# An RWKV kernel on one core: output matrices built on VectorE, head loads on SyncE, and a re-placed end of the state chain

## The chip, the core and the metric

The kernel runs on one core of a Trainium2 chip. A core has a matrix engine (TensorE, PE in the profile; its weight loads are shown as PEld), VectorE (DVE), ScalarE (ACT), GpSimd (POOL) and SyncE (SP). Each engine works through its own queue in order, and the engines wait for each other by semaphores. SP, ACT and POOL can issue DMAs. The metric is the device time of one execution in microseconds; lower is better.

## What is computed

A recurrence over time runs for each of 16 sequences of 2048 steps and each of 256 channels. `k` and `v` are 16 x 2048 x 256 floats (33.5 MB each), and so is the output.

```python
for t in range(seq_len):
    ww = u + kk                       # kk = k[b,t], vv = v[b,t]
    qq = np.maximum(pp, ww)
    e1 = np.exp(pp - qq); e2 = np.exp(ww - qq)
    output[b, t] = (e1 * aa + e2 * vv) / (e1 * bb + e2 + 1e-08)
    ww = pp - w + kk
    qq = np.maximum(ww, kk)
    e1 = np.exp(ww - qq); e2 = np.exp(kk - qq)
    aa = e1 * aa + e2 * vv
    bb = e1 * bb + e2
    pp = qq
```

The output is a decayed sum of values (the numerator) over a decayed sum of weights (the denominator); `aa`, `bb` and `pp` carry the state.

## The kernel before

**Tiling.** 2048 = 32 + 16 x 126. The first 32 steps of all sequences are "the head"; the rest are 16 steps of time, c = 0 to 15, of 126 rows each (two halves of 63). A tile has the time on its partitions. The work is cut into 66 pairs: a pair is one step of time of 4 sequences (two matrix tiles of 512 columns). Pairs 0 and 1 belong to step 0, pairs 2 and 3 are the head (pair 3 is half as large), pairs 4 and 5 finish step 0, and then there are four pairs for each step: pairs 58 to 61 are step 14, pairs 62 to 65 are step 15.

**One pair.** Its K and V are loaded (`load`, 512 KB each; four buffers of each). DVE casts K (`round_k`, writing `km`, L285). PE multiplies it by two constant matrices (`logs`, L301, writing `X`), ACT takes exponentials (`exps`, L317, writing `ez`), V is cast to bf16 (`cast_v`; on ACT for pairs 2 to 7, L326, otherwise on DVE, L328), DVE multiplies `ez` by V (`times_v`, L336), and PE adds up columns (`sums`, L366, writing `tot`). Ten rounds later (six for the head) comes the output of the pair: PE makes denominators (`den`, L512) and numerators (`num`, L534) with the constant matrices `Lf`, `Id`, `LfN`, `IdN` (`Lh`, `LhN` for the head); ACT takes the logarithm of the denominators (`log_den`, L521) and the exponential of its negative (`invert`, L526); DVE multiplies (`mult`, L542); and a DMA stores the tile (`store`, L562). From pair 8 on `X` has one buffer of four PSUM banks, so `logs` of the next pair waits for `exps` of this one.

**The state chain.** When the four pairs of a step are summed, a chain of small instructions turns sums into the carries of that step: ACT copies `tot` (`copy_sums`, `ts`), PE transposes it (`turn_sums`, L382), DVE copies that (`split_sums`, `tsum`, L389), ACT takes logarithms (`state_logs`, `lf`, L401), DVE adds and clamps them (`state_offset`, L406; `state_near`, `near`, L410), ACT makes weights from these (`state_weights`, `w` and `g`, L420 and L421), DVE updates the state (`state_sums`, `state_add`, `state_decay`), ACT makes two more small functions (`inject_logs` `y`, L455; `inject_weights` `phi`, L461), DVE forms the carries (`carry_weights`, `carries` `ab`, L466 and L473), PE transposes them (`turn_carries`, L479, with the matrix `It`), DVE copies them (`row`, L484), and SP sends them by four small DMAs of 8 KB into two spare rows of `ez` (`inject`, L488). Denominators and numerators of the step's pairs read these rows.

**The order.** The order on each engine is the order in which the program is written: the helper `K` pins each instruction behind the one before it on its engine. The main loop has rounds n = 0 to 77; in round n it does `exps`, `times_v` and `sums` of pair n, the cast and `logs` of pair n + 1, `den` and `log_den` of pair q = n - 10, `invert` of n - 11, and `num`, `mult` and `store` of n - 12. Between these stand named slots (`a0` to `a4`, `d0` to `d5`, `p0` to `p4`), where `small_work` puts pieces of the state chain and of the set-up; a table `PLANS` says for each kind of step, counted in rounds from its last pair, which piece goes into which slot. Slot `a3` is ahead of `exps(n)`, `d5` and `a1` stand at the end of a round, `d2` behind the first `mult`. From round 66 on there are no new pairs, and `widen` gives the freed PSUM banks to denominators (two buffers) and numerators (three).

**Set-up.** POOL makes the base matrices `M1` and `I1`. From these POOL also builds the output matrices, in three batches, at the ends of rounds 3, 4 and 5 (L253 to L256, L260 to L263, L267 to L273), between the loads that it issues. Loads of pairs 0 and 1 are on SP, those of pairs 4 and later on POOL, four pairs ahead. The head's loads are small pieces of 32 rows, K on SP and V on POOL (L129). All stores are on POOL, but for the second half of the last pair's, on SP.

Of the kernel before, what the change touches and what calls it, by code (L numbers as in the profile page):

```python
# [7 lines left out]
F32 = mybir.dt.float32  # L8
F32R = mybir.dt.float32r
BF16 = mybir.dt.bfloat16  # L10
ALU = mybir.AluOpType
# [11 lines left out]
def kernel(  # L23
# [11 lines left out]
    def K(ins):  # L35

        block, e, new = nc.cur_bb.bb, ins.ins.engine, []
        for i in reversed(block.instructions):
            if i.engine == e:
                new.append(i)  # L40
                if i.name == pinned.get(e):
                    break
        for a, b in zip(new[1:], new):
            tc.add_manual_dep(b, a.name, mybir.DependencyInfo(
                mybir.DependencyClass.NoSync, mybir.DependencyReason.DATA), reason="order")
        pinned[e] = new[0].name
# [12 lines left out]
    NH = NG * GB  # L59
# [5 lines left out]
    RS = 2.0 ** -43  # L65
# [30 lines left out]
    NP = len(pairs)  # L96
# [17 lines left out]
    def load(n):  # L114
        kr = kpool.tile([128, 4, Dm], F32, tag="kr", name="kr")
        vr = vpool.tile([128, 4, Dm], F32, tag="vr", name="vr")
        kr_of[n], vr_of[n] = kr, vr
        c, p = pairs[n]
        if is_head(n):
            if p == 1:  # L120
                K(POOL.memset(kr[64:96, 0:2, :], 0.0))
                K(POOL.memset(vr[64:96, 0:2, :], 0.0))

            for t, x, eng, groups in ((kr, k, SP, range(NG)), (vr, v, POOL, reversed(range(NG)))):
                for g in groups:
# [26 lines left out]
    def matrix(name, dt, width=128):  # L152
        return consts.tile([128, width], dt, tag=name, name=name)
# [7 lines left out]
    def fill(ap, value):  # L161
        K(DVE.memset(ap.bitcast(F32) if ap.dtype == F32R else ap, value))
# [3 lines left out]
    cc = matrix("cc", F32, 8)  # L166
# [18 lines left out]
    def head_blocks(f):  # L185
        fill(f[0:GB, GB:NH], 0.0)
        fill(f[GB:2 * GB, 2 * GB:NH], 0.0)
# [62 lines left out]

    def matrices_for_outputs():

        K(POOL.tensor_copy(It, I1))  # L253
        K(POOL.tensor_copy(Id, I1))
        K(POOL.tensor_copy(Id[:, TC:128], I1[:, TC - 1:TC].broadcast_to([128, 128 - TC])))
        K(POOL.tensor_scalar(IdN, Id, RS, None, ALU.mult))  # L256

    def matrices_for_outputs_of_head():
        for t, s in ((Lh, 1.0), (LhN, RS)):
            K(POOL.tensor_scalar(t, M1, -s, None, ALU.mult))  # L260
            K(POOL.memset(t[0:GB, GB:NH], 0.0))
            K(POOL.memset(t[GB:2 * GB, 2 * GB:NH], 0.0))
            K(POOL.memset(t[:, NH:128], 0.0))  # L263

    def more_matrices_for_outputs():
        Lx = matrix("Lx", F32)
        K(POOL.tensor_scalar(Lx, M1, -1.0, None, ALU.mult))  # L267
        K(POOL.memset(Lx[0:HS, HS:TC], 0.0))
        K(POOL.tensor_scalar(Lx[:, 0:HS], Lx[:, 0:HS], cc[:, 2:3], None, ALU.add))
        K(POOL.tensor_scalar(Lx[:, HS:TC], Lx[:, HS:TC], cc[:, 3:4], None, ALU.add))  # L270
        K(POOL.tensor_copy(Lx[:, TC:128], Lx[:, TC - 1:TC].broadcast_to([128, 128 - TC])))
# [235 lines left out]
    def den(n):  # L507
        rl, ri = (NH, NH) if is_head(n) else (128, TC)
        d = bank("den", [128, 2, D])
        for m, r, q in (((Lh if is_head(n) else Lf), rl, 0), (Id, ri, 2)):  # L510
            for i in range(tiles_of(n)):
                K(PE.matmul(d[:, i, :], m[0:r, :], ez_of(n)[0:r, q, i, :], start=q == 0, stop=q == 2,  # L512
                            skip_group_check=True))
        DEN[n] = d
# [29 lines left out]
    def store(n):  # L544
        o = RD.pop(n).rearrange("p i (n d) -> p (i n) d", n=2)
        if n % 2 == 1:
            EZ.pop(n // 2)
        if is_head(n):
            for g in range(NG):
                b = 6 * g + 4 * pairs[n][1]  # L550
                e = min(b + 2 * tiles_of(n), B)
                if b < e:
                    K(POOL.dma_start(out=out[b:e, 0:T0, :].rearrange("n t d -> t n d"),
                                     in_=o[g * GB:(g + 1) * GB, 0:e - b, :]))
        else:
# [18 lines left out]
    def small_work(n, where):  # L574
        for f, args in later.pop((n, where), []):
            f(*args)
# [13 lines left out]
                   (3, "d4", state_decay, 0), (4, "a0", inject_logs), (4, "a2", inject_weights),  # L590
                   (4, "d4", carry_weights), (4, "d5", carries), (4, "p4", turn_carries), (5, "d0", inject),
                   (5, "d2", state_add, 1), (5, "d4", state_decay, 1)),
        "last": ((1, "a0", copy_sums), (1, "p1", turn_sums), (1, "p1", split_sums), (1, "a2", state_logs),
                 (1, "d5", state_offset, 0), (1, "d5", state_offset, 1), (1, "d5", state_near),
                 (1, "a1", state_weights), (2, "d0", state_sums), (2, "d0", state_add, 0),
                 (2, "d0", state_decay, 0), (2, "a2", inject_logs), (2, "a2", inject_weights),
                 (2, "d2", carry_weights), (2, "d2", carries), (2, "p2", turn_carries), (2, "d5", inject)),
    }
    for c in range(-1, NST):
        for slot, where, f, *args in PLANS["head" if c < 0 else "first" if c == 0 else  # L600
                                           "last" if c + 1 == NST else "steady"]:
# [12 lines left out]
    for n in range(NP + LAG + 2):  # L614

        q, qi, qp = out_at.get(n), out_at.get(n - 1), out_at.get(n - 2)
        live, more, out_q, out_qi, out_qp = n < NP, n + 1 < NP, q is not None, qi is not None, qp is not None
        if n == NP:
            widen()
        if n + AHEAD < NP:  # L620
            load(n + AHEAD)
        small_work(n, "a3")
        if live:
            exps(n)
        small_work(n, "d0")
# [75 lines left out]
```

## Time and profile before

| | |
|---|---|
| times of five runs | 323.63, 324.89, 325.53, 327.46, 330.95 us |
| median | 325.53 us |
| the profiled execution's own time | 323.63 us |
| its span, first to last instruction | 321.9 us |
| mean granted TensorE clock | 0.978 |
| moved by DMA | 102.96 MB, 320 GB/s over the span |

The profile is of the fastest of the five runs; 1.7 us of its time lie outside the span. In the rows of the profile a label such as L512 is a line of the kernel, `out<-in` are tile names, and a bracket at the end gives how long the engine had been idle before and what ended that. PEclk is the granted TensorE clock in tenths.

### The profile page before, as it was taken

What the parts mean: (1) busy time and instruction counts of PE and PEld (TensorE: products, weight loads), DVE (VectorE), ACT (ScalarE), POOL (GpSimd) and SP (SyncE); (2) the same over time, 40 slices, a digit from 0 to 9 for tenths busy, and PEclk for the clock granted to TensorE, in tenths of its full rate; (3) what the DMA queues carried; (4) which work ended last, traced back from release to release, by engine and by line L of the source; (5) the groups of instructions that cost most, each with busy time, mean ns of one, the idle gap of its engine ahead of it and who ended that gap; (6) DMA issues with size and microseconds to landing.
All of it is one profiled execution on the core that took longest, in us unless ns stands there. A gap on an engine that the chain in (4) does not pass through costs nothing. (4 is left out here: it accounts for less than half of the span.)

```text
span 321.9 us, 3974 instructions
## 1 busy us (share of the span) xinstructions
PE 281.1 (87%) x1132; PEld 126.4 (39%) x1132; DVE 277.6 (86%) x546; ACT 278.3 (86%) x318; POOL 179.2 (56%) x249
## 2 busy tenths in 40 slices
PE   1699779799999999999999999999999999997980
PEld 1334334254444444344444344444434444432430
DVE  4847877989999999999999999999999999977670
ACT  6589689599898999989898989899998989986990
POOL 8778917564466655556664646665555664112331
PEclk9999799999999999999999999999999999997995
DMA  6999798999999999999999999999999999944775
GB/s 205 245 349 350 227 340 243 328 337 320 344 348 356 377 359 363 352 365 365 372 357 347 375 360 368 363 374 357 347 370 369 368 318 279 312 166 155 246 250 171
DMA packets 33743, 102.96 MB, mean 320 GB/s; under 512 B 6638, under 2 KB 9482, under 8 KB 33722
## 3 DMA queue, kind: packets, MB, share of 16 engines
q0 software_dynamic: 27616, 99.27, 90.1%
q1 hardware_dynamic: 6074, 3.42, 4.2%
q8 instruction: 9, 0.15, 0.2%
q14 instruction: 12, 0.10, 0.1%
q10 hardware_dynamic: 32, 0.02, 0.0%
HBM read 68.12 MB, written 34.05 MB: 317 GB/s over the span
## 5 line engine op out<-in xcount | busy, mean ns | idle before, releaser
L562 POOL DMA_DIRECT2D out_dram<-rd x64 | 53.8, 841 | 121.3 <-issue 48.3
L317 ACT ACTIVATE ez<-X 128x2048 bf16<-128x2048 f32 x58 | 108.6, 1873 | 8.7 <-PE num L534 6.7
L542 DVE TENSOR_TENSOR rd<-num,rd 128x512 f32<-128x512 f32 (+2 forms) x131 | 88.9, 685 | 15.8 <-ACT rd L526 6.7
L336 DVE TENSOR_TENSOR ez<-ez,vb 126x2048 bf16<-126x2048 bf16 (+1 forms) x66 | 79.7, 1207 | 6.4 <-ACT ez L315 5.8
L521 ACT ACTIVATE rd<-den 128x1024 f32<-128x1024 f32 (+3 forms) x67 | 67.0, 1000 | 16.5 <-PE den L512 16.1
L526 ACT ACTIVATE rd<-rd 128x1024 f32<-128x1024 f32 (+3 forms) x67 | 69.3, 1034 | 0.3
L301 PE MATMUL X<-km,NLE 128*128 128x512 f32 x128 | 52.2, 490 | 10.2 <-DVE km L285 6.5
L135 POOL DMA_DIRECT2D kr<-in_k_dram x62 | 56.5, 912 | 2.5 <-DVE km L285 1.4
L534 PE MATMUL num<-ez,LfN 128*128 128x512 bf16 x128 | 49.6, 388 | 4.4 <-DVE rd L542 0.8
L534 PE MATMUL num<-ez,IdN 126*128 126x512 bf16 (+1 forms) x131 | 50.3, 384 | 0.0
L135 POOL DMA_DIRECT2D vr<-in_v_dram x62 | 48.6, 785 | 2.5 <-ACT vb L326 1.6
L328 DVE CAST vb<-vr 126x1024 bf16<-126x1024 f32 x60 | 46.6, 776 | 0.8 <-DMA vr<-in_v_dram 0.7
L366 PE MATMUL tot<-ez,OHV 126*48 126x512 bf16 x128 | 39.3, 389 | 7.7 <-DVE ez L336 6.3
L285 DVE CAST km<-kr 126x1024 fp32r<-126x1024 f32 x64 | 43.9, 687 | 1.9 <-DMA kr<-in_k_dram 1.9
L301 PE MATMUL X<-km,NLZ 128*128 128x512 f32 x128 | 41.4, 406 | 0.4 <-ACT ez L315 0.2
L512 PE MATMUL den<-ez,Lf 128*128 128x512 bf16 x128 | 38.5, 382 | 2.4 <-DMA ez<-row 1.6
L366 PE MATMUL tot<-ez,OHE 128*48 128x512 bf16 x128 | 40.5, 399 | 0.0
L512 PE MATMUL den<-ez,Id 126*128 126x512 bf16 (+1 forms) x131 | 39.4, 381 | 0.0
L301 PEld LDWEIGHTS X<-km,NLE 128*128 128x128 f32 x128 | 23.8, 192 | 22.3 <-DVE km L285 6.5
L301 PEld LDWEIGHTS X<-km,NLZ 128*128 128x128 f32 x128 | 24.6, 194 | 7.4 <-ACT ez L315 1.7
L366 PEld LDWEIGHTS <-OHV 126*48 126x48 bf16 x128 | 13.5, 105 | 30.2 <-issue 21.5
L534 PEld LDWEIGHTS <-LfN 128*128 128x128 bf16 x128 | 12.4, 97 | 28.9 <-issue 26.0
(111 smaller groups left out, 215.1 us busy)
## 6 DMA issues: line engine op xcount, KB each, us to landing
out_dram<-rd POOLq DMA_DIRECT2D x60, 512.0 KB, 7.1
kr<-in_k_dram POOLq DMA_DIRECT2D x58, 512.0 KB, 8.1
vr<-in_v_dram POOLq DMA_DIRECT2D x58, 512.0 KB, 8.6
kr<-in_k_dram POOLq DMA_DIRECT2D x4, 504.0 KB, 10.3
vr<-in_v_dram POOLq DMA_DIRECT2D x4, 504.0 KB, 11.0
out_dram<-rd POOLq DMA_DIRECT2D x3, 504.0 KB, 4.3
kr<-in_k_dram SPq DMA_DIRECT2D x2, 512.0 KB, 5.0
vr<-in_v_dram SPq DMA_DIRECT2D x2, 512.0 KB, 7.8
```

The lines of the kernel that those rows point to most:

```text
L135: K((SP if n < 2 else POOL).dma_start(out=t[0:r, :, :], in_=x[4 * p:4 * p + 4, t0:t0 + r, :].rearrange("n t d -> t n d")))
L301: K(PE.matmul(X[q][:, i, :], m[0:kr, :], km[0:kr, i, :], start=True, stop=True))
L317: K(SC.activation(ez_of(n)[:, 0:4:2], X[2][:, :, 0:i, :], ACT.Exp))
L328: K(DVE.tensor_copy(vb[0:r, 0:i, :], vr_of.pop(n)[0:r, 0:i, :]))
L336: K(DVE.tensor_mul(ez[0:r, 1:4:2], ez[0:r, 0:4:2], vb[0:r, 0:i, :].unsqueeze(1).broadcast_to([r, 2, i, D])))
L366: K(PE.matmul(TOT[c], m[0:r, :], ez_of(n)[0:r, q, i, :], start=n == first_of[c] and i == 0 and q == 0, stop=n == last_of[c] and i == tiles ...
L512: K(PE.matmul(d[:, i, :], m[0:r, :], ez_of(n)[0:r, q, i, :], start=q == 0, stop=q == 2, skip_group_check=True))
L521: K(SC.activation(RD[n][0:r, a:b, :], DEN[n][0:r, a:b, :], ACT.Ln, scale=RS))
L526: K(SC.activation(RD[n][0:r, a:b, :], RD[n][0:r, a:b, :], ACT.Exp, scale=-1.0))
L534: K(PE.matmul(d, m[0:r, :], ez_of(n)[0:r, q, i, :], start=q == 1, stop=q == 3, skip_group_check=True))
L542: K(DVE.tensor_mul(RD[n][0:r, i, :], NUM.pop((n, i))[0:r, :], RD[n][0:r, i, :]))
L562: K(eng.dma_start(out=out[4 * p + a:4 * p + b, t0:t0 + r, :].rearrange("n t d -> t n d"), in_=o[0:r, a:b, :]))
```

## The change

Four things change.

1. The output matrices are built on DVE instead of POOL, at the same places of the loop (ends of rounds 3, 4 and 5), with 15 instructions instead of 19; the float32 stage `Lx` is gone.
2. The head's loads all go to SP, K and then V of pair 2, K and then V of pair 3.
3. In the state chain, step 14 has a plan of its own ("before"), mostly one round earlier than "steady" had it: the copy of sums at the end of round 62, `lf` ahead of `exps(63)`, the carries sent in round 65. In the plan of step 15 ("last") offsets and `near` come behind the first product of round 66 instead of the second, and the carries' weights, the carries and their transposition at the end of round 67, behind both products and the denominators.
4. In round 66 the second numerator comes behind `turn_sums`; in round 67 the denominators of pair 58 come directly behind those of pair 57. The store of pair 64 goes to SP.

```diff
-            for t, x, eng, groups in ((kr, k, SP, range(NG)), (vr, v, POOL, reversed(range(NG)))):
-                for g in groups:
+            for t, x in ((kr, k), (vr, v)):
+                for g in range(NG):
...
-                        K(eng.dma_start(out=t[g * GB:(g + 1) * GB, 0:e - b, :],
+                        K(SP.dma_start(out=t[g * GB:(g + 1) * GB, 0:e - b, :],
...
     def matrices_for_outputs():
-        K(POOL.tensor_copy(It, I1))
-        K(POOL.tensor_copy(Id, I1))
-        K(POOL.tensor_copy(Id[:, TC:128], I1[:, TC - 1:TC].broadcast_to([128, 128 - TC])))
-        K(POOL.tensor_scalar(IdN, Id, RS, None, ALU.mult))
+        K(DVE.tensor_copy(It, I1))
+        K(DVE.tensor_copy(Id[:, 0:TC], I1[:, 0:TC]))
+        K(DVE.tensor_copy(Id[:, TC:128], I1[:, TC - 1:TC].broadcast_to([128, 128 - TC])))
+        K(DVE.tensor_single_scalar(IdN, Id, RS, op=ALU.mult))
     def matrices_for_outputs_of_head():
-        for t, s in ((Lh, 1.0), (LhN, RS)):
-            K(POOL.tensor_scalar(t, M1, -s, None, ALU.mult))
-            K(POOL.memset(t[0:GB, GB:NH], 0.0))
-            K(POOL.memset(t[GB:2 * GB, 2 * GB:NH], 0.0))
-            K(POOL.memset(t[:, NH:128], 0.0))
+        K(DVE.tensor_single_scalar(Lh, M1, -1.0, op=ALU.mult))
+        head_blocks(Lh)
+        fill(Lh[:, NH:128], 0.0)
+        K(DVE.tensor_single_scalar(LhN, Lh, RS, op=ALU.mult))
     def more_matrices_for_outputs():
-        Lx = matrix("Lx", F32)
-        K(POOL.tensor_scalar(Lx, M1, -1.0, None, ALU.mult))
...
-        K(POOL.tensor_copy(Lf, Lx))
-        K(POOL.tensor_scalar(LfN, Lx, RS, None, ALU.mult))
+        K(DVE.tensor_single_scalar(Lf, M1, -1.0, op=ALU.mult))
+        fill(Lf[0:HS, HS:TC], 0.0)
+        K(DVE.tensor_scalar(Lf[:, 0:HS], Lf[:, 0:HS], cc[:, 2:3], None, ALU.add))
+        K(DVE.tensor_scalar(Lf[:, HS:TC], Lf[:, HS:TC], cc[:, 3:4], None, ALU.add))
+        K(DVE.tensor_copy(Lf[:, TC:128], Lf[:, TC - 1:TC].broadcast_to([128, 128 - TC])))
+        K(DVE.tensor_single_scalar(LfN, Lf, RS, op=ALU.mult))
...
-            for a, b, eng in ((0, 2, POOL), (2, 4, SP)) if n == NP - 1 else ((0, 4, POOL),):
+            for a, b, eng in ((0, 2, POOL), (2, 4, SP)) if n == NP - 1 else ((0, 4, SP if n == NP - 2 else POOL),):
...
+        "before": ((1, "a0", copy_sums), (1, "p2", turn_sums), (1, "d5", split_sums), (2, "a3", state_logs),
+                   (2, "d1", state_offset, 0), (2, "d2", state_offset, 1), (2, "d3", state_near),
+                   (2, "a1", state_weights), (3, "d0", state_sums), (3, "d1", state_add, 0),
+                   (3, "d1", state_decay, 0), (3, "a0", inject_logs), (3, "a2", inject_weights),
+                   (3, "d4", carry_weights), (3, "d5", carries), (3, "p4", turn_carries), (4, "d0", inject),
+                   (4, "d2", state_add, 1), (4, "d4", state_decay, 1)),
...
-                 (1, "d5", state_offset, 0), (1, "d5", state_offset, 1), (1, "d5", state_near),
+                 (1, "d2", state_offset, 0), (1, "d2", state_offset, 1), (1, "d2", state_near),
...
-                 (2, "d2", carry_weights), (2, "d2", carries), (2, "p2", turn_carries), (2, "d5", inject)),
+                 (2, "d5", carry_weights), (2, "d5", carries), (2, "a1", turn_carries), (2, "a1", inject)),
...
         if out_qp:
             num(qp, 0)
-            if not live:
+            if n > NP:
                 num(qp, 1)
...
         small_work(n, "p1")
+        if n == NP:
+            num(qp, 1)
...
         if out_q:
-            den(q)
+            if q not in DEN:
+                den(q)
+            if n == NP + 1:
+                den(q + 1)
```

More of the change, by code (lines that the diff above doesn't have):

```diff
@@ L251, in matrices_for_outputs @@
     def matrices_for_outputs():
-        K(POOL.tensor_copy(It, I1))
-        K(POOL.tensor_copy(Id, I1))
-        K(POOL.tensor_copy(Id[:, TC:128], I1[:, TC - 1:TC].broadcast_to([128, 128 - TC])))
-        K(POOL.tensor_scalar(IdN, Id, RS, None, ALU.mult))
+        K(DVE.tensor_copy(It, I1))
+        K(DVE.tensor_copy(Id[:, 0:TC], I1[:, 0:TC]))
+        K(DVE.tensor_copy(Id[:, TC:128], I1[:, TC - 1:TC].broadcast_to([128, 128 - TC])))
+        K(DVE.tensor_single_scalar(IdN, Id, RS, op=ALU.mult))
     def matrices_for_outputs_of_head():
-        for t, s in ((Lh, 1.0), (LhN, RS)):
-            K(POOL.tensor_scalar(t, M1, -s, None, ALU.mult))
-            K(POOL.memset(t[0:GB, GB:NH], 0.0))
-            K(POOL.memset(t[GB:2 * GB, 2 * GB:NH], 0.0))
-            K(POOL.memset(t[:, NH:128], 0.0))
-    def more_matrices_for_outputs():
-        Lx = matrix("Lx", F32)
-        K(POOL.tensor_scalar(Lx, M1, -1.0, None, ALU.mult))
[L268 to L271, printed above, removed]
-        K(POOL.tensor_copy(Lf, Lx))
-        K(POOL.tensor_scalar(LfN, Lx, RS, None, ALU.mult))
+        K(DVE.tensor_single_scalar(Lh, M1, -1.0, op=ALU.mult))
+        head_blocks(Lh)
+        fill(Lh[:, NH:128], 0.0)
+        K(DVE.tensor_single_scalar(LhN, Lh, RS, op=ALU.mult))
+    def more_matrices_for_outputs():
+        K(DVE.tensor_single_scalar(Lf, M1, -1.0, op=ALU.mult))
[4 more added lines that the diff above has]
+        K(DVE.tensor_single_scalar(LfN, Lf, RS, op=ALU.mult))
     EZ, X_of, KM = {}, {}, {}
@@ L600 @@
         for slot, where, f, *args in PLANS["head" if c < 0 else "first" if c == 0 else
-                                           "last" if c + 1 == NST else "steady"]:
+                                           "last" if c + 1 == NST else "before" if c + 2 == NST else "steady"]:
             at(last_of[c] + slot, where, f, c, *args)
```

## The prediction

> **What bounds the kernel now.** I read the busy shares first, then the stages, then the waits, and last the timeline at both ends.
>
> ```profile
> PE 281.1 (87%) x1132; PEld 126.4 (39%) x1132; DVE 277.6 (86%) x546; ACT 278.3 (86%) x318; POOL 179.2 (56%) x249
> ...
> PEclk9999799999999999999999999999999999997995
> ...
> 80.00:120.00 40.00, 37.68 (x161) 17.47 (x160) 38.37 (x74) 36.85 (x41) 23.36 (x29) 1.00 1.02 356
> ...
> 280.00:290.00 10.00, 9.44 (x41) 3.90 (x40) 7.80 (x17) 8.43 (x13) 2.26 (x3) 1.00 0.53 190
> 290.00:300.00 10.00, 7.74 (x30) 3.06 (x29) 6.83 (x19) 7.04 (x11) 2.26 (x3) 0.83 0.53 173
> ```
>
> Three engines share the work, and none idles in the middle: of 40 us DVE is busy 38.4 and ACT 36.9 (columns: PE, PEld, DVE, ACT, POOL, clock, DMA share, GB/s). No edit touches rounds 6 to 61, so I cost the middle at nothing. At the ends there is room: in 290 to 300 us ACT works 7.0 of 10 us and the TensorE clock is 0.83. The chain that ended last runs through ACT from 297.78 us on, in steps of 2.0 us per pair.
>
> ```profile
> ACT vb L326 <- DMA vr<-in_v_dram: 2.5, 1, 2.5
> ...
> PE den L512 <- DMA ez<-row: 1.6, 1, 1.6
> ...
> 273.84 1.87 ACT L317 ACTIVATE ez<-X 128x2048 bf16<-128x2048 f32 x1
> ...
> 275.75 0.35 DVE L389 COPY tsum<-den 128x192 f32<-128x192 f32 x1
> ...
> 276.54 0.26 ACT L401 ACTIVATE lf<-tsum 128x64 f32<-128x64 f32 x1
> ...
> 289.49 0.26 ACT L401 ACTIVATE lf<-tsum 128x64 f32<-128x64 f32 x1 [0.87 <-DVE tsum L389]
> ...
> 290.06 1.02 ACT L521 ACTIVATE rd<-den 128x1024 f32<-128x1024 f32 x1 [0.32 <-PE den L512]
> ...
> 291.64 0.26 ACT L420 ACTIVATE w<-near 128x64 f32<-128x64 f32 x1 [0.56 <-DVE near L410]
> ...
> 294.18 0.29 PE L479 MATMUL num<-It,ab 128*128 128x128 bf16 x1 [2.18 <-DVE ab L473]
> ...
> 297.78 1.02 ACT L521 ACTIVATE rd<-den 128x1024 f32<-128x1024 f32 x1 [2.24 <-PE den L512]
> ```
>
> The first two rows are the only waits for DMA that matter: ACT for the V of pair 2 (until 15.38 us) and PE at 46.67 us for the first carries. The rest is the end. ACT waits 0.87 + 0.32 + 0.56 + 2.24 = 4.0 us: the most that a better order can give there. Before 297.78 PE had waited 2.18 us for the last carries, with the denominators of pair 58 queued behind them.
>
> **The change, part by part.**
>
> *Matrices on DVE.* POOL loses 19 instructions, DVE gains 15, in rounds 3, 4 and 5. From the nearest DVE rows (128x126 scale 0.29 us, 48x48 cast 0.18, 63x63 memset 0.11, 128x96 clamp 0.2): round 3 0.8 us, round 4 0.85, round 5 (six, each waiting for the last) 1.35; 3.0 in all. DVE idled 2.10 us before 24.19, 0.54 + 0.37 before 27.42 and 0.96 before 30.30: rounds 3 and 4 fit. Round 5 does not: the cast of pair 7 (28.56) moves to 29.9, its logs on PE (29.48) to 30.6, then the sums of step 0, DVE's copy (31.74 to 32.2), ACT's logarithm behind it, and so exp(7) from 32.28 to 32.8: **+0.5**. Bounds: 0 (the casts there took 0.77 to 0.88 us beside a working POOL, 0.68 elsewhere) and +0.9.
>
> *Loads freed on POOL.* POOL issued pair 10's K at 33.30, behind matrices; its buffer is free after the cast at 26.8, so the load comes some 6 us sooner, and POOL's next ones too. No engine waited for those. But they were issued as one lump (eight in 33.3 to 39.3), just as the first carry rows went out at 38.47; these landed behind them, and PE waited until 46.67 (row two). Spread out, the rows meet a shorter queue; at the 6.2 us that such a row usually takes they land by 45.7.
>
> *Head loads on SP alone.* Five V chunks go behind K on SP, at 0.43 us each; nothing else is queued on SP until 38.47. But each needs a free completion slot of eight: pair 2's last V chunk waits for V of pair 0 (7.1 us), K of pair 3 for pair 1's K and V (8.8 and 11.2), V of pair 3 for K of pair 2 (to 12). POOL meanwhile issues K and V of pair 4 at 6.4 and 7.9 (before 10.2 and 11.0) and K of pair 5 at 9.6: 1.57 MB that are not urgent. In order of issue, 3.4 MB must land for pair 2's V with K of pair 4, 3.95 with its V: 1.65 MB come in the first slice (205 GB/s), the rest at 245 to 300: between 13.9 and 17.4, I take 15.7, that is 0.4 late. Pair 3's chunks come behind 4.6 MB: K at 19.0, V near 20. Then exp(3) starts at 20.8 instead of 19.67, and exp(4), which had 0.51 us to wait, at 22.8 instead of 22.21: **+0.5**, bounds 0 and +3. The rule against this edit: the Trainium skill, DMA: Bandwidth & Descriptors, "Queues, rings and completion order", lets each DMA engine take turns between queues, packet by packet. POOL's packets average 3.6 KB (99.27 MB in 27616), SP's head packets are 1 KB, so POOL would take four fifths, pair 2's V comes after 17.5 and the head loses 1 us more. The trace disagrees: an 8 KB carry row takes 6.2 us to land, far more than a few turns, so it stands behind what was issued. I take the row.
>
> *Head sum.* exp(8) is 1.0 late, the carry rows leave at 39.5, PE reaches pair 0's denominators at 45.07 + 1.0 = 46.1, rows landed, instead of 46.67; ACT takes their logarithm at 46.48 + 1.0 = 47.5 instead of 47.74. **-0.25**, bounds -1.2 and +3.5.
>
> *State chain of step 14, one round earlier.* Its first ACT step, lf, now stands ahead of exp(63). lf needs the copy of sums (275.75, end 276.1), which needs pair 62's sums on PE. So ACT, free at 273.84, waits until 276.2: a **new stall of 2.35 us**. Queued behind it on ACT are exp(63) (now 276.4), inverse 52 and log 53; DVE's product with V and PE's logs of pair 64 wait for exp(63). DVE too idles 0.5 for the copy, now ahead of pair 64's cast. Down the chain (X has one buffer): logs(64) 278.3 (were 276.83), exp(64) 280.3 (278.59), logs(65) 282.3, exp(65) 284.4 (283.09), last sums done 288.6 (287.05). Step 14's later pieces sit in gaps of PE, DVE and ACT. Its carry rows leave at 285.9, two us sooner.
>
> *Last chain and pair 58.* With one numerator after it, the turn of the last sums goes at 289.3 (288.44), lf at 290.4, denominators 56 done 291.3, log at 291.4 (290.06): still 1.3 late. But near is ready, so w and g follow at once (0.56 saved); inverse 56, y, phi; log 57 at 294.15 (293.45). PE does denominators 58 right after 57, by 293.9, with rows landed by about 290; ACT logs pair 58 at **296.2 instead of 297.78: -1.55**, and keeps its 2.0 us steps: denominators 59 are done at 298.1 and due at 298.2. The carries, now behind two products on DVE, turn at 295.2 and land by 300, for pair 62 due near 304.
>
> Here the second rule counts. The Trainium skill, TensorE: Matmul & The Clock Gate, Part 1, puts the half clock behind an idle window of about 3.4 us; by it a 2.18 us gap costs nothing. The trace shows 0.83, and matmuls of 0.63 us instead of 0.38 from 294.26 to 297.6: eight at 0.21 extra, some 1.5 us. By the rule the tail would gain 0.05; by the row 1.55. I take the row. Whether the other runs had this half clock one profile can't tell; without it the gain is 1.5 less (324.7). The new gap on PE is 293.9 to 295.2, 1.3 us in one window, and I expect full clock.
>
> *Last stores.* POOL starts a store 0.6 us after its product (product done 313.2, issue 313.81), SP 0.03 after (314.92, 314.95). Pair 64 on SP starts 0.6 sooner, and POOL's half of pair 65 isn't queued behind it; both transfers share the DMA engines, so the end gains **-0.55**, bounds 0 and -1.0.
>
> Sum: -0.25 - 1.55 - 0.55 = **-2.35 us** on the profiled execution's own 323.63: 321.3, or 0.7% less. The runs' median is 325.53, so I predict **323.2**.
>
> **The rivals.** *All gains, no costs* (chance 0.28): V lands on time, round 5 hides, so the head gives its 1.2; the tail also gets back half of the stall, 0.8; stores 1.0: -4.55, 321.0. For it: ACT's 4 us of waits, the 1.6 us on PE. Against: lf's place ahead of exp(63) is fixed by the order. *Head V late* (0.22): place, the cast of pair 2 and pair 3 on ACT; price, up to +3 at exp(4) if pairs 4 and 5 move first, all carried on, since the carry rows then leave 3.5 us later and land as late; +3.5 - 2.1 = +1.4: **326.9**. It decides once the head loses over 2.1 us, pair 2's V after about 18.3. For it: ACT waits there already. Against: SP's ring is filled before POOL's. A third, *the early denominators wait for their rows*, would undo the tail's gain; rows two rounds ahead speak against it, and I leave it inside the forecast.
>
> **Numbers.** Forecast 0.50: 323.2, its own range 321.7 to 324.9. A measurement of this kernel tells about 1% (3.3 us) from no change. Over 1% faster is most of the first rival and an edge of the forecast: 0.30. Over 1% slower needs the late V at its worst or a second half-clock window: 0.14. The rest is 0.56. Range 319.9 to 327.1: from the first rival's reach to the second's.
>
> **What would show it.** Right: ACT idle some 2.3 us before exp(63); no wait over 0.5 us on ACT after 292; log 58 1 to 2 us sooner; clock near 1.0 in 290 to 300; exp(4) and exp(8) up to 1 us late; the 46.67 wait below 0.6; DVE 3 us busier. Wrong: exp(4) 2 us late or more, half clock again near 295, or a middle that is no longer 4.4 us per pair.

## The result, and the profile after

The changed kernel takes **322.72 us** in the median of 43 runs (319.78 to 330.37), the kernel before 325.51 us in 74 runs. The ratio is **0.9958**, with a 95% interval of 0.9935 to 0.998: the change saves 0.4%, which is clear of zero but inside the 1% that the prediction gave as no change. The prediction was 323.2 us, from a sum of -0.7%. So the total came out close; the parts did not all do so. One of them missed by 2 us at its own place, and a wait took up more than half of that.

The ratio compares only the runs within 1.5% of the fastest of each kernel, which is why it is nearer to 1 than the two medians are (0.991), and the profiled execution, at 324.94 us, is not among these, so I read where its steps stand and not how long it is. First its page and its table by stage (columns as before: length, then PE, PEld, DVE, ACT, POOL with the number of instructions, clock, DMA share, GB/s):

```profile
PE 279.3 (86%) x1132; PEld 126.6 (39%) x1132; DVE 278.0 (86%) x561; ACT 278.4 (86%) x318; POOL 166.6 (52%) x224
...
PEclk9999999999999999999999999999999999999996
```

```profile
80.00:120.00 40.00, 37.72 (x161) 17.43 (x160) 38.37 (x74) 37.33 (x42) 23.42 (x29) 1.00 1.01 350
...
290.00:300.00 10.00, 8.54 (x40) 3.67 (x39) 7.56 (x20) 8.77 (x15) 2.26 (x3) 1.00 0.52 175
```

DVE has its 15 instructions more, POOL 25 fewer. The clock is full until 318 us; before, it was 0.83 in 290 to 300. In that slice ACT now works 8.8 of 10 us instead of 7.0. The middle is as it was.

The waits tell of the head:

```profile
ACT vb L322 <- DMA vr<-in_v_dram: 5.6, 2, 4.0
...
ACT rd L517 <- DMA out_dram<-rd: 4.2, 3, 1.6
...
DVE kmh L281 <- DMA kr<-in_k_dram: 3.9, 1, 3.9
```

The wait of PE for the carry rows (1.6 us before) is gone, but the waits for the head's data are longer, and waits for stores are new. The timeline of ACT, at the head, ahead of `exps(63)` and at the end, where 296.57 and 298.57 are the logarithms of pairs 57 and 58:

```profile
17.60 1.06 ACT L322 ACTIVATE vb<-vr 96x1024 bf16<-96x1024 f32 x1 [3.99 <-DMA vr<-in_v_dram]
...
22.08 0.63 ACT L322 ACTIVATE vb<-vr 96x512 bf16<-96x512 f32 x1 [1.60 <-DMA vr<-in_v_dram]
22.61 1.06 ACT L311 ACTIVATE ez<-X 128x512 bf16<-128x512 f32 x2
...
24.74 1.94 ACT L311 ACTIVATE ez<-X 128x1024 bf16<-128x1024 f32 x2
```

```profile
275.53 1.02 ACT L517 ACTIVATE rd<-den 128x1024 f32<-128x1024 f32 x1 [1.42 <-DMA out_dram<-rd]
277.66 0.26 ACT L397 ACTIVATE lf<-tsum 128x64 f32<-128x64 f32 x1 [1.10 <-DVE tsum L385]
277.82 1.86 ACT L313 ACTIVATE ez<-X 128x2048 bf16<-128x2048 f32 x1
...
296.57 1.00 ACT L517 ACTIVATE rd<-den 128x1024 f32<-128x1024 f32 x1
...
298.57 1.00 ACT L517 ACTIVATE rd<-den 128x1024 f32<-128x1024 f32 x1
```

V of pair 2 comes at 17.60 us (15.38 before, 15.7 forecast) and exp(4) at 24.74 (22.21 before, 22.8 forecast): 2.5 us late. At the other end, pair 58's logarithm stands right behind pair 57's with no wait, where it had waited 2.24 us. From the start of exp(65) to the start of that logarithm it takes 298.57 - 287.19 = 11.4 us; before, 297.78 - 283.09 = 14.7. But exp(65) itself is late here: it follows exp(62) by 16.4 us (before, 13.4), with waits of 1.42 and 1.15 us for stores on ACT beside the forecast wait for `lf`. So from exp(62) to pair 58's logarithm this execution takes 27.75 us, only 0.4 less than before (28.1).

### The profile page after: what moved, and what is told of

The parts are those of the page before. It is cut to its first block, busy times and chain, and to the rows that moved or that the text cites. A ratio compares the mean times of both kernels' runs of the same rounds, so it can differ in the third digit from the quotient of the medians.

```text
span 323.2 us, 3968 instructions
## 1 busy us (share of the span) xinstructions
PE 279.3 (86%) x1132; PEld 126.6 (39%) x1132; DVE 278.0 (86%) x561; ACT 278.4 (86%) x318; POOL 166.6 (52%) x224
## 4 chain that ended last, share of the span: by engine, by line
DMA 16%; DVE 16%; ACT 15%; PE 11%; issue 5%; POOL 1%; ACTq 0%; DVEq 0%
ACT ez L313 8%; DMA vr<-in_v_dram 6%; DVE ez L332 6%; DMA out_dram<-rd 5%; DMA kr<-in_k_dram 4%; ACT rd L517 4%; DVE vb L324 3%; PE num L530 3%; DVE rd L538 3%; PE den L508 2%; ACT rd L522 2%; PE X L297 2%; DVE km L281 2%; PE tot L362 1%; PE den L378 1%
## 5 line engine op out<-in xcount | busy, mean ns | idle before, releaser
L558 POOL DMA_DIRECT2D out_dram<-rd x63 | 52.7, 837 | 119.7 <-ACT ez L313 28.0
L517 ACT ACTIVATE rd<-den 128x1024 f32<-128x1024 f32 (+3 forms) x67 | 67.0, 1000 | 16.2 <-PE den L508 11.6
L134 POOL DMA_DIRECT2D vr<-in_v_dram x62 | 50.0, 807 | 10.4 <-ACT vb L322 7.1
L324 DVE CAST vb<-vr 126x1024 bf16<-126x1024 f32 x60 | 45.6, 760 | 3.0 <-DMA vr<-in_v_dram 3.0
L362 PEld LDWEIGHTS <-OHV 126*48 126x48 bf16 x128 | 13.4, 104 | 31.6 <-issue 22.5
L530 PEld LDWEIGHTS <-LfN 128*128 128x128 bf16 x128 | 12.3, 96 | 28.5 <-issue 25.4
## 6 DMA issues: line engine op xcount, KB each, us to landing
vr<-in_v_dram POOLq DMA_DIRECT2D x58, 512.0 KB, 10.1
```

The lines of the kernel that those rows point to most:

```text
L134: K((SP if n < 2 else POOL).dma_start(out=t[0:r, :, :], in_=x[4 * p:4 * p + 4, t0:t0 + r, :].rearrange("n t d -> t n d")))
L324: K(DVE.tensor_copy(vb[0:r, 0:i, :], vr_of.pop(n)[0:r, 0:i, :]))
L362: K(PE.matmul(TOT[c], m[0:r, :], ez_of(n)[0:r, q, i, :], start=n == first_of[c] and i == 0 and q == 0, stop=n == last_of[c] and i == tiles ...
L517: K(SC.activation(RD[n][0:r, a:b, :], DEN[n][0:r, a:b, :], ACT.Ln, scale=RS))
L530: K(PE.matmul(d, m[0:r, :], ez_of(n)[0:r, q, i, :], start=q == 1, stop=q == 3, skip_group_check=True))
```

## Experiments

All ratios are to the kernel before. "Log 58" is the logarithm of pair 58's denominators, "exp(n)" the exponential of pair n. The runs e1, e2 and e3 change the kernel before by one part of the change each, and e5 adds useless work to it. e4 is the change without its head loads; e7, e8, e10 and e12 start from e4, and e6, e9 and e11 from the changed kernel.

### e1: the head loads alone

```diff
-for t, x, eng, groups in ((kr, k, SP, range(NG)), (vr, v, POOL, reversed(range(NG)))):
+for t, x in ((kr, k), (vr, v)):          # all on SP, K then V
```

> The kernel before with only the head's V loads moved to SyncE, behind K, as in the change. Theory A (late V): pairs 4 and 5, now issued early by GpSimd, land ahead of the V of pairs 2 and 3; exp(2) starts near 18.5 us (16.34 before), exp(4) near 24.7 (22.21), exp(8) near 38.5 (36.04), and the logarithm of pair 0's denominators near 48.5 (47.74): the run is 0.5 to 1.3 us longer than before. Rival B (covered): the lateness is the same up to exp(8), but the wait of 1.6 us for the carry rows takes it up; the logarithm of pair 0 starts by 47.9 and the time is within 0.3 us of before.

Measured: 324.82 us, ratio 1.0011 (0.9972 to 1.005). exp(2) starts at 19.05, exp(4) at 25.27, exp(8) at 39.79 and pair 0's logarithm at 50.05, 2.3 us later than before. The lateness is that of theory A, and it does reach pair 0's denominators, though this execution also had the half clock for 10 us (20.5 to 30.8), which adds to it. The time resolves nothing.

### e2: the output matrices alone

```diff
-K(POOL.tensor_copy(It, I1)) ...          # three batches, 19 instructions
+K(DVE.tensor_copy(It, I1)) ...           # three batches, 15 instructions
```

> The kernel before with only the output matrices moved from GpSimd to VectorE. Theory A (on the path): exp(4) unchanged at 22.2, exp(7) 0.5 to 0.9 us later than 32.28, and pair 0's logarithm as much later than 47.74: the time is 0.5 to 0.9 us longer. Rival B (the freed queue pays for it): exp(7) is as late, but GpSimd's loads are spread out, the carry rows land sooner, the wait of 1.6 us at pair 0's denominators shrinks below 0.8, and pair 0's logarithm starts at 47.4 to 47.7: the time is 0 to 0.4 us shorter.

Measured: 325.21 us, ratio 1.0015 (0.9963 to 1.0066). exp(2) was 2.4 us late here, at 18.73 (K of pair 1 came 1.1 us late), although the head's code was the old one: the landing of the head's data varies between executions. So I count from exp(4): exp(7) follows it by 10.63 us, by 10.07 before. The carry rows leave 1.4 us later than before, yet PE waits for them 0.23 us instead of 1.61, and pair 0's logarithm starts at 47.77 (47.74 before). Rival B, in kind: the rows came 6.8 us after they left, 8.2 before, and took up the lateness. What changed on the queue is seen in the table by stage, first before, then e2:

```profile
32.00:36.00 4.00, 2.33 (x8) 1.05 (x7) 3.40 (x10) 3.00 (x7) 3.93 (x7) 0.83 0.45 114
```

```profile
32.00:36.00 4.00, 2.69 (x12) 1.53 (x12) 3.30 (x8) 3.11 (x5) 2.32 (x3) 1.00 1.03 347
```

In these 4 us POOL had been busy for 3.93 with matrices, and the DMA engines, with no loads to do, stood at 0.45; now they are full. That this is what brings the rows sooner is not shown: e4 has the same matrices, and its rows take 8.0 us again.

### e3: the end alone

```diff
+"before": (... (1, "d5", split_sums), (2, "a3", state_logs), ...)    # step 14
...
-(1, "d5", state_offset, 0) ...  (2, "d2", carries), (2, "p2", turn_carries)
+(1, "d2", state_offset, 0) ...  (2, "d5", carries), (2, "a1", turn_carries)
...
+if n == NP + 1:
+    den(q + 1)
...
-... else ((0, 4, POOL),)
+... else ((0, 4, SP if n == NP - 2 else POOL),)
```

> The kernel before with only the end of the change: both chains' places, pair 58's denominators ahead of the last carries, pair 64 stored by SyncE. Theory A (order): from the start of exp(65) to the start of pair 58's logarithm it takes 11.4 us instead of 14.7, exp(65) starts about 1 us later than before because of the new wait ahead of exp(63), and the time is 1.5 to 2.5 us shorter. Rival B (only the half clock of before's profiled execution was lost): in most executions of before the pass from exp(65) to that logarithm is already near 13 us, so the time is 0.5 us shorter or less.

Measured: 323.84 us, ratio **0.9962** (0.9927 to 0.9997). ACT's timeline:

```profile
276.33 0.26 ACT L401 ACTIVATE lf<-tsum 128x64 f32<-128x64 f32 x1 [2.28 <-DVE tsum L389]
276.49 1.86 ACT L317 ACTIVATE ez<-X 128x2048 bf16<-128x2048 f32 x1
...
291.41 1.02 ACT L521 ACTIVATE rd<-den 128x1024 f32<-128x1024 f32 x1 [0.76 <-PE den L512]
...
294.12 1.00 ACT L521 ACTIVATE rd<-den 128x1024 f32<-128x1024 f32 x1
...
296.12 1.00 ACT L521 ACTIVATE rd<-den 128x1024 f32<-128x1024 f32 x1
```

Theory A at its places; the time saved, 0.4% or 1.2 us, is a little under its 1.5 to 2.5. This is the cleanest test of the prediction's steps, because its exp(62) (269.84) stands within 0.2 us of before's (269.65): the stall was forecast as 2.35 us and is 2.28; exp(63), exp(64), exp(65) were forecast at 276.4, 280.3, 284.4 and are 276.49, 280.42, 284.41; the logarithms of pairs 56, 57, 58 at 291.4, 294.15, 296.2 and are 291.41, 294.12, 296.12. It is also the best case. In the six profiles with this end (e3, e4, e6, e9, e10 and the changed kernel) log 58 follows exp(62) by 26.3 to 27.75 us, e3 being the lowest; in the three with the old one (before, e1, e2) by 27.7 to 28.5.

### e4: all but the head loads

Against the changed kernel:

```diff
-for t, x in ((kr, k), (vr, v)):          # all on SP
+for t, x, eng, groups in ((kr, k, SP, range(NG)), (vr, v, POOL, reversed(range(NG)))):
```

> The changed kernel with the head loads as before (V on GpSimd, last group first). Theory A (the head loads are the one part that costs): exp(4) is back at 22.2, pair 0's logarithm starts at 47.4 to 47.9, and the time is 0.8 to 1.3 us below the changed kernel's, 2 to 3 us below before's. Rival B (the wait for the carry rows comes back in their place): pair 0's denominators wait again for their rows, the logarithm starts at 48.5 or later, and the time is that of the changed kernel, 1.4 us below before.

Measured: 321.58 us, ratio **0.9938** (0.991 to 0.9967), 0.2% below the changed kernel's 0.9958; the two intervals overlap widely. exp(4) starts at 21.36 and pair 0's logarithm at 46.53, 1 us sooner than theory A had it, after a wait of 1.40 us for the rows. Theory A is right about the place; the time decides nothing.

### e5: TensorE kept busy in the gap

In the kernel before, ahead of the turn of the last carries:

```diff
+for i in range(10 if c + 1 == NST else 0):
+    K(PE.matmul(d[:, 128:512].rearrange("p (a x) -> p a x", a=3), Id,
+                Id.unsqueeze(1).broadcast_to([128, 3, 128]), start=True, stop=True))
 K(PE.matmul(d[:, 0:128], st.pop((c, "ab")).rearrange("p m q x -> p (m q x)"), It, ...))
```

> The kernel before with ten useless matmuls of 384 columns on TensorE (0.16 us each, 1.6 us in all), put right before the turn of the last carries, where TensorE idled 2.18 us; they write columns of the bank that nothing reads. Theory A (the idle gap brings the half clock): the clock in 290 to 300 us is near 1.0 instead of 0.83, the matmuls behind the turn take 0.38 us instead of 0.63, pair 58's logarithm starts 14.7 - 1.5 = 13.2 us after exp(65), and the time is about 1.5 us shorter although TensorE does more. Rival B (the half clock comes from something else): the clock stays at 0.83, the pass from exp(65) to that logarithm stays at 14.7 us, and the time is within 0.3 us of before.

Measured: 325.37 us, ratio 0.9985 (0.995 to 1.002). The matmul behind the turn in the kernel before, then two views of e5, PE's timeline and the table by stage:

```profile
294.26 0.63 PE L534 MATMUL num<-ez,LfN 128*128 128x512 bf16 x1
```

```profile
294.22 1.79 PE L480 MATMUL num<-Id 128*128 128x384 bf16 x10
296.57 0.23 PE L482 MATMUL num<-It,ab 128*128 128x128 bf16 x1 [0.57 <-DVE ab L473]
296.64 0.38 PE L537 MATMUL num<-ez,LfN 128*128 128x512 bf16 x1
```

```profile
290.00:300.00 10.00, 9.36 (x48) 4.30 (x46) 7.46 (x21) 7.43 (x13) 3.01 (x4) 1.00 0.45 145
```

The filler fills the gap, the clock stays full, and the matmul behind the turn takes 0.38 us instead of 0.63. Log 58 follows exp(65) by 13.5 us instead of 14.7: 1.2 us gained at that step by useless work. Theory A holds for the mechanism, 0.3 us short in size; in the time of whole runs it can't be told from nothing.

### e6: pairs 4 and 5 in the same queue

```diff
-K((SP if n < 2 else POOL).dma_start(
+K((SP if n < 6 else POOL).dma_start(
```

> The changed kernel with the loads of pairs 4 and 5 on SyncE too, so that they stand in one queue behind the head's K and V. Theory A (pairs 4 and 5 from GpSimd's queue take the DMA engines from the head's V): exp(2) starts near 16.3 us instead of 18.57, exp(4) near 22.2 instead of 24.74, exp(11) 1 to 2 us sooner than 49.77, and the time is 0.8 to 1.5 us below the changed kernel's. Rival B (SyncE's own waits for completion slots make the V late): its chunks leave SyncE as before, up to 13.4 us, exp(2) stays near 18.5, exp(4) near 24.5, and the time is that of the changed kernel or longer.

Measured: 326.66 us, ratio 1.004 (1.0009 to 1.0071): slower than before. V of pair 2 ends its wait at 16.99, exp(2) starts at 19.12. Neither theory fits whole. V is little sooner although nothing stands beside it, and the table by stage shows the DMA engines nearly idle:

```profile
14.00:16.00 2.00, 1.70 (x4) 0.32 (x3) 1.37 (x8) 1.84 (x2) 0.00 (x0) 1.00 0.14 32
```

SP stands in its waits for completion slots (its last head loads leave at 16.3), and all of pairs 4 and 5 is queued behind them; exp(5) comes at 31.02 (28.01 in the changed kernel). K of pair 1 also came late in this execution (its cast starts at 11.83, 8.89 before), so e6 does not decide between the theories. e9 was made for that.

### e7: lf back behind exp(63)

In e4's plan of step 14:

```diff
-(1, "d5", split_sums), (2, "a3", state_logs), (2, "d1", state_offset, 0),
+(2, "d1", split_sums), (2, "a2", state_logs), (2, "d2", state_offset, 0),
```

> The kernel with the head loads as before and all else changed (e4), but step 14's logarithm lf put behind exp(63), where the steady plan has it, with the copy of its sums and its offsets behind it. Theory A (the stall ahead of exp(63) is a true cost): exp(63) starts some 2.5 us sooner in respect of exp(62), exp(65) some 1.3 us, pair 58's logarithm as much, and the time is 0.8 to 1.3 us below e4's. Rival B (the stall only moved slack that the tail has anyway, or step 14's later pieces now hold up the last chain): ACT waits elsewhere before pair 58's logarithm and the time is within 0.3 us of e4's.

Measured: 321.61 us, ratio **0.9912** (0.9874 to 0.9949). exp(63) follows exp(62) by 4.1 us instead of 6.6, and log 58 follows exp(62) by 25.5 instead of 26.9. The median is e4's (321.58). The step gains what theory A says in this execution, the whole run doesn't show it; see e12, where the step doesn't show it either.

### e8: pair 58's denominators in their own turn

```diff
-if q not in DEN:
-    den(q)
-if n == NP + 1:
-    den(q + 1)
+den(q)
```

> e4 with pair 58's denominators back in their own turn, behind the last carries. Theory A (their early place is the gain of the end): ACT waits 1.5 to 2.5 us for them again, pair 58's logarithm starts 13 us or more after exp(65) instead of 11.8, and the time is 1.2 us or more above e4's. Rival B (the earlier chain is the gain, the order only follows): with the carries turned sooner the denominators are done when ACT is free, the wait is below 0.5 us, and the time is within 0.4 us of e4's.

Measured: 322.45 us, ratio 0.9972 (0.994 to 1.0004), 0.9 us above e4 in the median; the intervals overlap.

```profile
296.90 1.02 ACT L518 ACTIVATE rd<-den 128x1024 f32<-128x1024 f32 x1 [0.99 <-PE den L509]
```

The wait is back, at 0.99 us, and log 58 starts 12.8 us after exp(65) instead of 11.8 in e4. It lies between the two theories: of the 2.9 us that the pass lost (14.7 to 11.8), the early denominators are worth 1.0, and the chain's new place with the full clock the other 1.9. The clock deserves a look: TensorE idled 2.09 us ahead of the turn of the last carries here, nearly as long as the 2.18 us before, and yet the clock stayed full (see the last chain below).

### e9: GpSimd's loads held back

In the changed kernel, ahead of the load of pair 4:

```diff
+if n == 4:
+    K(POOL.tensor_copy(cc[0:96, 6:7], vr_of[2][0:96, 3, Dm - 1:Dm]))
```

> The changed kernel with one more GpSimd instruction ahead of its first load: it copies a column of pair 2's V, so that the loads of pairs 4 to 7 are issued only once that V has landed. In the changed kernel's profile the two queues land packet for packet from 15 to 20 us (65 of GpSimd's 4 KB to 66 of SyncE's 1 KB in one us). Theory A (that turn-taking keeps pair 2's V until 17.6): with nothing beside it V lands by 15, exp(2) starts at 16 or sooner instead of 18.57, exp(4) unless pair 4's own K is late near 22. Rival B (SyncE's waits for completion slots, and a slow end of the chunks themselves, hold it): V lands at 16.5 to 17.5 all the same, with the DMA engines idle in 14 to 16 us, and exp(2) starts near 18. Either way pair 4's loads start 7 to 9 us later than 7.13, so the whole may be longer than the changed kernel's.

Measured: 323.77 us, ratio 1.001 (0.9958 to 1.0062). POOL's first instruction behind its wait, then ACT's timeline:

```profile
14.21 1.08 POOL L116 COPY cc<-vr 96x1 f32<-96x1 f32 x1 [7.95 <-DMA vr<-in_v_dram]
```

```profile
14.15 1.06 ACT L324 ACTIVATE vb<-vr 96x1024 bf16<-96x1024 f32 x1 [1.22 <-DVE kmh L283]
15.76 1.94 ACT L313 ACTIVATE ez<-X 128x1024 bf16<-128x1024 f32 x2 [0.55 <-PE X L299]
...
18.44 1.08 ACT L313 ACTIVATE ez<-X 128x512 bf16<-128x512 f32 x2 [0.23 <-PE X L299]
...
21.26 1.06 ACT L324 ACTIVATE vb<-vr 126x1024 bf16<-126x1024 f32 x1 [1.73 <-DMA vr<-in_v_dram]
```

**Theory A.** With nothing beside it V of pair 2 has landed by 14.2 us, 3.4 us sooner than in the changed kernel, and exp(2) and exp(3) start 2.8 and 4.2 us sooner (18.57 and 22.61 there). SP's waits for slots are still in e9 and don't keep V. Held back so far, pair 4's own V is late (the last row), and this execution had the half clock from 24.2 to 27.6 us, so exp(8) gains only 1.3 us (37.78 against 39.05). And then the end of the head takes even that, in PE's timeline:

```profile
47.66 0.38 PE L510 MATMUL den<-ez,Lf 128*128 128x512 bf16 x1 [1.38 <-DMA ez<-row]
```

The rows leave at 39.68, 1.3 us sooner than in the changed kernel, and PE starts pair 0's denominators at 47.66 where the changed kernel started them at 47.39. This fits a time that does not move. It is one execution; e11, held back for a shorter while, has exp(2) at 15.89 again.

### e10: the store of pair 64 on GpSimd

```diff
-... else ((0, 4, SP if n == NP - 2 else POOL),)
+... else ((0, 4, POOL),)
```

> e4 (all of the change but the head loads) with the store of pair 64 on GpSimd as before. Theory A (its place on SyncE gains what the sum had): from the end of ACT's last instruction to the end of the span it takes 0.5 us more than e4's 7.3 us (319.7 - 312.4), and the time is 0.5 us longer. Rival B (the two last transfers share the DMA engines, so that an earlier start of one changes nothing): within 0.15 us of it.

Measured: 321.97 us, ratio 0.9975 (0.9918 to 1.0031). From the end of ACT's last instruction to the end of the span it takes 7.47 us, in e4 7.33. Rival B: 0.14 us, within its 0.15. Over all profiles that stretch is 7.1 to 7.8 us with the store on SP and 7.5 to 7.9 with it on POOL.

### e11 and e12: the best of the runs

e11 is the changed kernel with `lf` as in e7 and POOL held back only until pair 2's K has landed; e12 is e7 again. Against e9, e11 has

```diff
-vr_of[2][0:96, 3, Dm - 1:Dm]
+kr_of[2][0:96, 3, Dm - 1:Dm]
```

and e7's edit.

> The changed kernel with two edits that the runs point to: GpSimd's first load is held back only until pair 2's K has landed (near 12 us, so that pair 4 follows the head's V without the gap of e9), and step 14's lf stands behind exp(63) as in e7. Theory A (both costs of the change are gone): exp(2) starts near 16, exp(4) near 22, pair 0's denominators start by 46.5 on TensorE, log 58 follows exp(62) by 25.5 us, and the time is 1.5 us or more below the changed kernel's 322.7 (ratio to before 0.991). Rival B (the carry rows take up what the head gains, as in e9): the head gains nothing at pair 0's denominators (47 us or later), and only the end's 1 us remains (ratio 0.993 or more).

> e7 once more, beside e11 on the same chip: the changed kernel with the old head loads and lf behind exp(63). Theory A (lf's place gains 1 us over e4): ratio to before 0.990 to 0.992, again log 58 25.5 us after exp(62). Rival B (e7's ratio of 0.991 was a lucky draw of few runs): 0.994 or more, as e4. The two kernels share head loads up to 20 us with e4, so exp(2) shows once more how far the landing of pair 2's V varies between executions (16.5 in e4, 19.0 in e7).

Measured: e11 322.11 us, ratio 0.998 (0.9948 to 1.0011); e12 321.56 us, ratio **0.9923** (0.9893 to 0.9953). e11 does at the head what theory A says (exp(2) at 15.89, exp(4) at 21.07, pair 0's denominators at 45.74 us), and its time is still no better than the changed kernel's. In both, log 58 follows exp(62) by 27 us and more (27.7 and 27.0), not by 25.5: the second step of theory A failed in both. ACT's timeline of e12 says why:

```profile
273.40 1.02 ACT L518 ACTIVATE rd<-den 128x1024 f32<-128x1024 f32 x1 [1.57 <-DMA out_dram<-rd]
...
277.02 0.26 ACT L398 ACTIVATE lf<-tsum 128x64 f32<-128x64 f32 x1
277.93 1.02 ACT L518 ACTIVATE rd<-den 128x1024 f32<-128x1024 f32 x1 [0.65 <-DMA out_dram<-rd]
```

`lf` no longer waits for its sums; instead two logarithms wait for stores to land, since they write into one of five output buffers that is still being stored. e7, e12 and e4 have medians within 0.05 us of each other and the lowest ratios (0.9912, 0.9923, 0.9938), but the interval of each overlaps the changed kernel's, e12's by 0.002. The change without its head loads may be the best version; these runs don't resolve it, nor whether `lf` behind exp(63) adds to it.

## Why the prediction was right, and where it was not

**The total** was right: 322.72 us against 323.2 in the median, and 0.4% saved against 0.7%. Of the parts, the head cost 1.4 us more than the sum had it, the stores gave 0.4 less, and the end up to log 58 was as forecast in the cleanest profile (e3). One term was put at nothing: behind log 58 ACT "keeps its 2.0 us steps", and with the new end the way from there to its last logarithm takes 15.3 to 15.9 us instead of the 15.2 before, with a wait ahead of pair 61's in most profiles; in e3 that is 0.4. Put together as measured the parts give +1.1 - 1.66 + 0.4 - 0.14 = -0.3 us, or 0.1%, less than the 0.2 to 0.65% of the interval, and they do not explain medians 2.8 us apart. So that the median came within 0.5 us of the forecast is in part luck. By the ratios the saving is that of the end: e3 alone has 0.9962, the whole change 0.9958, and the intervals of e1 and e2 hold 1.

**Matrices (+0.5).** Right in place, a little small. In the profiles with them on DVE whose loads are not held back or moved to SP (e2, e4, e7, e8, e10, e12 and the changed kernel) exp(7) follows exp(4) by 10.6 to 10.8 us; in the three at full clock with POOL's (before, e3, e5) by 10.0 to 10.1. That is +0.65. Round 5's six instructions take 1.03 us, not 1.35. The sign "DVE 3 us busier" failed (278.0 us against 277.6): the 15 instructions hold the engine for 2.3 us (0.57 + 0.74 + 1.03 in the changed kernel), but its casts of V take 1.0 us less (45.6 against 46.6), and the rest was not traced.

**Loads freed on POOL.** Right that the loads come sooner (pair 10's K is issued at 28.60 in e2, at 33.30 before); what that does to the rows stays open (6.8 us under way in e2, 8.0 in e4, 8.2 before). In 32 to 36 us of the kernel before the DMA engines stood at 0.45 because their issuer was computing; e2 shows them full. I counted only what the loads did to the rows.

**Head loads (+0.5; measured +2.5 at exp(4)).** This step failed, and the term is the landing of pair 2's V: 15.7 forecast, 17.60 measured. With it came the prediction's own sign of being wrong, "exp(4) 2 us late or more". The failed reasoning is "The trace disagrees ... I take the row". The rule that I set aside (the Trainium skill, DMA: Bandwidth & Descriptors, "Queues, rings and completion order": the engines take turns between queues, packet by packet) gave "after 17.5" for V, which is what came, and "1 us more" for the head, where 2 came; this case's trace fits the rule in the sum over some us. The DMA view of the changed kernel for 15 to 20 us alone, with packets, MB and share by queue (q0 POOL's, q1 SP's):

```profile
q0 software_dynamic: 363, 1.34, 86.3%
q1 hardware_dynamic: 312, 0.26, 19.6%
```

About one packet to one, and 1.34 of 1.60 MB, five sixths, to the queue with the large packets. It is not even: 69 to 63 in 15 to 16 us, 65 to 65 in 17 to 18, but 91 to 11 in 14 to 15. That GpSimd's loads hold V up is shown by e9 and e11, one profile each: they keep the loads away, and exp(2) starts at 15.8 and 15.9 instead of 18.6 (changed kernel) and 19.1 (e1), V 3.4 us sooner in e9. That the engines do it turn by turn fits and is not shown. Nor are these loads the only cause: in e6 nothing stood beside V, and it still came at 16.99, in an execution whose K of pair 1 was late. My row did not bear on the question: that an 8 KB row takes 6.2 us to land says how long a small transfer is under way, not how two backlogs share the engines.

One caution: the old head loads are not safe either. With them exp(2) started at 16.2 to 16.8 us in six profiles (before, e3, e4, e5, e8, e12) and at 18.7 to 20.5 in three (e2, e7, e10), each time with K of pair 1 late (cast at 9.9 to 11.1 us, 8.7 to 9.0 in the six). With all loads on SP and POOL not held back it was 18.6 to 19.1 in all three.

**Head sum (-0.25; measured +1.1).** Pair 0's logarithm starts at 48.86, 47.74 before. The wait for the rows took up lateness as forecast, only more: exp(8) is 3.0 us late (39.05 against 36.04, forecast 1.0), the log 1.1. In e9 and before the rows took 8 us from SP to PE; in the changed kernel, leaving 2.5 us later, they were there in less than 6.5. This is also why the rival **Head V late** did not come true in its price: its mechanism did happen, but it had the rows "land as late". At 8.2 us under way they would have come at 49.2, 2.5 us later than before; as it was, about 2 us of the 3 were taken up. Why the rows came faster the runs don't show.

**The stall (2.35).** Right: 2.28 in e3. In the changed kernel's own profile it is split, 1.42 for a store and 1.10 for the copy. That it is a cost is seen at the step in e7 (1.4 us) and not again in e11 and e12, where waits for stores came in its place; the time doesn't show it.

**The last chain and pair 58 (-1.55).** Right to 0.12 us at six places in e3. The other profiles with this end gain less from exp(62) to log 58, from 0.4 us (the changed kernel) to 1.2 (e4, e9). The second rule (the Trainium skill, TensorE: Matmul & The Clock Gate, Part 1: the half clock comes behind an idle window of about 3.4 us) was rightly set below the row: with PE idle 2.18 us in one piece, a half-clock stretch begins at 294.1 to 297.0 us in each of the three profiles with the old end and no filler (before, e1, e2), and in none of the other eleven; e5 shows that the gap brings it. What agrees with the page is the length: every half-clock stretch before the very end is 3.41 us long, or two or three times that. But the length of the gap alone does not decide, as e8 shows. The table by stage for the 3.41 us ahead of the half clock in the kernel before and for the stretch with the gap in e8, whose ends lie whole steps of 3.41 us ahead of e8's next change of clock (314.63 us):

```profile
290.65:294.06 3.41, 1.35 (x7) 0.39 (x4) 2.68 (x11) 2.82 (x7) 0.75 (x1) 1.00 0.39 126
```

```profile
290.74:294.15 3.41, 2.07 (x10) 0.73 (x8) 2.72 (x9) 3.01 (x7) 0.75 (x1) 1.00 0.46 157
```

PE was busy for 1.35 us of the one stretch (1.35 in e2, 1.23 in e1) and for 2.07 of the other: e8's gap of 2.09 us lay across the end of its stretch, and the half clock did not come. So a part of the saving is clock: e5 gains 1.2 of the 2.9 us by clock alone, without moving a step. The prediction wrote 1.5 for it; its own eight matmuls at 0.21 make 1.7.

**Last stores (-0.55).** Wrong: 0.14 in e10. That the last transfers share the DMA engines, which the prediction named, would explain it; no run separates that.

**The middle at nothing.** True to 0.1 us for the changed kernel: from exp(11) to exp(62) it takes 221.05 us, before 220.98. Over all fourteen profiles it is 220.2 to 221.9, so the middle alone moves a profile by up to 1 us either way. What I left out is the DMA share in the same rows, 1.02. It did not slow the middle, but near 272 to 282 us (share still 1.03 to 1.04 until 280) ACT's logarithms waited for stores in most profiles: 1.0 us in e2, 1.7 in e5, 2.2 in e12, 2.6 in the changed kernel, 2.8 in e11, nothing in before, e3, e4 and e8. That these waits take up what the head and `lf` gain in e11 and e12 fits their rows; no run took the stores away, so how large a floor they set stays open.

## What to carry to other kernels

When two DMA queues have backlogs at once, don't take the order of issue for the order of landing. Here the queue with the 4 KB packets got five sixths of the bytes, and urgent data in 1 KB pieces came over 2 us late, beside bulk loads that an issuer freed of other work had started sooner. A wait near the end of a stage can take up lateness from before it (2 of 3 us here) and earliness too (e9), so follow each gain or loss on to the next wait before adding it. And look at gaps on TensorE for the clock that they can cost the work behind them, not only for their own length: 2.18 us cost it here, 2.09 us in e8 did not.

## What the runs showed of the hardware that was not expected

- A gap of 2.18 us in one place, with TensorE otherwise at work, brought 3.41 us of half clock, three times of three; ten useless matmuls (1.79 us) in it kept the clock full, and so did, in e8, a gap of 2.09 us that lay across the end of a 3.41 us stretch.
- The head's pieces themselves were slow: in 10 to 12 us of the changed kernel, with nothing from GpSimd landing, the DMA engines were full (share 1.15) at 218 GB/s, where the same 1 KB packets of pairs 0 and 1 had gone at 379 GB/s in 4 to 6 us (share 1.08). These pieces go to 32 partitions each, those loads to 126; no run tells whether that is the cause.
- The same head loads gave exp(2) at 16.2 to 20.5 us, yet pair 0's denominators at 45.4 to 48.5: part of the spread is gone by then, some of it in waits for the rows (1.61 us before, 0.23 in e2).
